# Two-layer decoder trunk: the end of the plain FFN columns as background streams, and the token sums in lanes of their own

## The chip, the cores and the metric

The kernel runs on one core of one Trainium2 chip. The metric is the time of one execution in microseconds (us), the median of three runs. All arithmetic is in 32-bit floats; the matmuls read them in a reduced fp32 form (fp32r), so every factor is split into a high and a low part and a product takes three passes.

## The reference

A trunk of two layers (l = 0, 1) works on 512 tokens of width 1024. In each layer stand an FFN half step (f = 0), a mixer, and another FFN half step (f = 1). The change touches the FFNs alone, and of these the part up to the first few of their 22 columns:

```
mod = c_act @ ada_w[l] + ada_b[l]          # nine vectors: shift, scale, gate
u = modulate(rmsnorm(h, ln_ffn), sh, sc)   # 512 x 1024
f = (silu(u @ w_gate) * (u @ w_up)) @ w_down     # 1024 -> 2816 -> 1024
h = h + 0.5 * gt * f
```

## The kernel before

**Tiling.** Activations stand transposed: 8 tiles of 128 features x 512 tokens. D_FF = 2816 is 22 columns of 128. Of the first columns of an FFN each is two plain products (`dense`: gate and up, 24 matmuls of 128x512 each, into one PSUM bank each, `mm`); the columns after them go in pairs by a scheme of seven products in place of eight (`dense_pair`), whose tokens stand in two halves of 256. A plain column ends in tanh on ACT (tile `t`), two VectorE instructions (`g` = (t+1)*gate, `ay` = g*up), and the split of `ay` into `ah` (a copy on ACT) and `al` (a subtraction on VectorE), which only the down product reads, behind the pairs.

**The pair.** Each of the seven jobs of `dense_pair` is 12 matmuls of 128x256: four k with the high parts, four with the low weight (`wl`), four with the low token part. The jobs use three banks X, Z and Y in the order X, Z, X, Y, X, Z, X. Jobs 1, 4 and 6 read `us` (the normalised tokens), jobs 2, 3, 5 and 7 read token sums `ts` (`th` high, `tl` low). After the first job ACT copies X into `c1` (in the trace `c<-mX`), and the third job, which overwrites X, waits for this copy.

**The token sums.** `halves_sums` makes them for k = 0 to 3: `make(0)` those of k = 0 and 2 on POOL, `make(1)` those of k = 1 and 3 on VectorE; per k four subtractions or additions and one sign change (`ta`, `tb`, 128x256), two copies on ACT (`th`, 128x512) and two subtractions on VectorE whatever the k (`tl`, 128x512). It is called at the end of `start()` (the first FFN; it also leaves the eight `mm` banks of four plain columns, `pss`) and of `tail()` (the others; two columns). The eight PSUM banks are all in use there, so the next `dense` needs a bank that one of these columns gives back: the first two banks are free when VectorE has done the column's two instructions.

**What sets the order.** The order on each engine is that in which the program text issues. After every third matmul (sixth in a pair) `tick()` makes one round through `lanes`, lists of generators, and steps those that a model clock calls due; in "post" it steps every due generator of the list, in the other lanes only the first due one. The lanes are gone through in the order in which the dictionary has them. `drain(names)` steps all lanes until the named ones are empty. The token sums stand in "post". `ffn()` begins with the four (or two) ready columns: all tanhs, all VectorE pairs, all splits. Then its loop goes through `seq`: for a "gu" column it makes the two `dense` and issues the column's end at once, in line; at the first "pair" it drains "post" and so the sums. In FFN (0,0) two plain columns (4 and 5) run in this loop, in the other three also two (2 and 3).

**Beside this** each weight tile is made into `wh` (copy on ACT) and `wl` (subtraction on VectorE) ahead of its use; POOL adds up weights of the pairs (`ws`); `ad`, `ca` and `ct` are the adaLN vectors, in work beside the FFNs.

Of the kernel before, what the change touches and what calls it, by code (L numbers as in the profile page):

```python
# [11 lines left out]
AF = mybir.ActivationFunctionType  # L12
OP = mybir.AluOpType
# [27 lines left out]
def ffn_order(first):  # L41


    seq = [("gu", i) for i in range(first)]
    nxt = first
    for ci, (lo, hi) in enumerate(CHUNKS):
        while nxt < min(hi + 1, FF):
            seq.append(("pair", nxt))
            nxt += 2
        seq.append(("down", ci))  # L50
    return seq


def first_gu(l, f):
    return 6 if (l, f) == (0, 0) else 4
# [3 lines left out]
def trunk(ctx: ExitStack, tc: tile.TileContext, x, c, ada_w, ada_b, ln, w_gu, w_dn, w_in, w_ba, conv_w,  # L59
# [17 lines left out]
    def big(s, shape=(128, 512), dt=F32):  # L77
        return bigp.tile(list(shape), dt, name=nm(s), tag="big")
# [46 lines left out]
    V, A, P, T = (Engine(k_, e_) for k_, e_ in zip("VAPT", (nc.vector, nc.scalar, nc.gpsimd, nc.tensor)))  # L125
# [43 lines left out]
    c_load()  # L169


    lanes = {"post": [], "dn0": [], "dn1": [], "at": []}

    def step(lane):

# [21 lines left out]
    def run(lane, gen):  # L197
        lanes[lane].append([gen, 0.0])
# [6 lines left out]
    def drain(*names):  # L205
        while any(lanes[n] for n in names):
            t = clock["T"]
            for n in lanes:
                step(n)
            if clock["T"] == t:  # L210
                clock["T"] += 100
# [380 lines left out]
            V.tensor_tensor(out=u[1][:, sl], in0=y, in1=u[0][:, sl].bitcast(F32), op=OP.subtract)  # L592
        return y, low

    def halves_sums(ys):

        lo, hi = HALF
        h12 = dnp.tile([128, 4, 2, 256], F32R, name=nm("th"), tag="MT")
        l12 = dnp.tile([128, 4, 2, 256], F32R, name=nm("tl"), tag="W")
        h34 = [dnp.tile([128, 2, 2, 256], F32R, name=nm("th"), tag=t_) for t_ in ("bt", "R")]  # L600
        ts = [[None] * 4 for _ in range(4)]

        l34 = [None] * 4

        def make(k0):
            for k in range(k0, 4, 2):
                l34[k] = big("tl", (128, 2, 256), F32R)
                for q, (th, tl) in enumerate(((h12[:, k], l12[:, k]), (h34[k // 2][:, k % 2], l34[k]))):
                    for i in range(2):
                        ts[2 * q + i][k] = (th[:, i, :], tl[:, i, :])  # L610
                E = (P, V)[k0]
                a, b = big("ta", (128, 2, 256)), big("tb", (128, 2, 256))
                y0, y1 = ys[k], ys[k + 4]
                E.tensor_tensor(out=a[:, 0, :], in0=y0[:, lo], in1=y0[:, hi], op=OP.subtract)
                E.tensor_tensor(out=a[:, 1, :], in0=y1[:, hi], in1=a[:, 0, :], op=OP.add)
                E.tensor_tensor(out=b[:, 1, :], in0=a[:, 1, :], in1=y1[:, lo], op=OP.subtract)
                yield
                E.tensor_scalar(out=a[:, 1, :], in0=a[:, 1, :], scalar1=-1.0, scalar2=None, op0=OP.mult)
                E.tensor_tensor(out=b[:, 0, :], in0=y1[:, hi], in1=y0[:, hi], op=OP.subtract)
                yield  # L620
                for t, th, tl in ((a, h12[:, k], l12[:, k]), (b, h34[k // 2][:, k % 2], l34[k])):
                    A.activation(out=th, in_=t, func=AF.Copy)
                    V.tensor_tensor(out=tl, in0=t, in1=th.bitcast(F32), op=OP.subtract)
                    yield

        for k0 in range(2):
            run("post", make(k0))
        return ts

    def pull(gen, n=1):  # L630
# [156 lines left out]
    def start(l, keys):  # L787
# [32 lines left out]
        y1s, us, ws, pss, ys = [], [], [], [], []  # L820
# [67 lines left out]
            V.tensor_tensor(out=sel, in0=sel, in1=ident[:, g:g + 16], op=OP.add)  # L888
        w_fill()
        w_ahead(12)  # L890
        return us, pss, halves_sums(ys)

    def split(y, s):
        hi, lo = big(s + "h", dt=F32R), big(s + "l", dt=F32R)
        A.activation(out=hi, in_=y, func=AF.Copy)
        V.tensor_tensor(out=lo, in0=y, in1=hi.bitcast(F32), op=OP.subtract)
        return hi, lo


    def ffn(l, f, us, pss, ts, nxt):  # L900
        act = {}
        st.update(ahead=AHEAD, raw=4)
        ada.update(rate=0.13, stop=min(len(ada_seq), 144 * l + 96 * f + 80))
        if (l, f) != (0, 0):
            ada["rate"] = 0.0
            c_load()

            def late():
                for _ in range(24):
                    yield False  # L910
                c_silu()
                ada["rate"] = 0.13

            run("post", late())
        seq = ffn_order(first_gu(l, f))

        def gate(cs, done):

            for c_, sign in zip(cs, (0.5, -0.5)):
                t = big("t")  # L920
                A.activation(out=t, in_=c_, func=AF.Tanh, scale=sign)
                yield
                V.scalar_tensor_tensor(out=c_, in0=t, scalar=1.0, in1=c_, op0=OP.add, op1=OP.mult)
                done.append(c_)
                yield

        def product(i, gs, done, ups):
            for j, (c_, y) in enumerate(zip(gs, ups)):
                while len(done) <= j:
                    yield False  # L930
                V.tensor_tensor(out=y, in0=c_, in1=y, op=OP.mult)
                yield
                act[i + j] = split(y, "a")
                yield
        gt = None
        there = [(pss[2 * i], pss[2 * i + 1]) for i in range(len(pss) // 2)]
        tanhs, ys = [big("t") for _ in there], [big("ay") for _ in there]
        for (pg, _), t in zip(there, tanhs):
            A.activation(out=t, in_=pg, func=AF.Tanh, scale=0.5)
        for (pg, pu), t, y in zip(there, tanhs, ys):  # L940
            V.scalar_tensor_tensor(out=t, in0=t, scalar=1.0, in1=pg, op0=OP.add, op1=OP.mult)
            V.tensor_tensor(out=y, in0=t, in1=pu, op=OP.mult)
        for i, y in enumerate(ys):
            act[i] = split(y, "a")
        for kind, i in seq[len(there):]:
            if kind == "gu":
                pg, pu = (dense(("gu", l, f, i, q), us) for q in range(2))
                t = big("t")
                A.activation(out=t, in_=pg, func=AF.Tanh, scale=0.5)
                g2 = big("g2")  # L950
                V.scalar_tensor_tensor(out=g2, in0=t, scalar=1.0, in1=pg, op0=OP.add, op1=OP.mult)
                y = big("ay")
                V.tensor_tensor(out=y, in0=g2, in1=pu, op=OP.mult)
                act[i] = split(y, "a")
            elif kind == "pair":
                if i == first_gu(l, f):
                    drain("post")
                g2s = dense_pair([("pair", l, f, j, 0) for j in (i, i + 1)], us, ts)
                done = []
                run("post", gate(g2s, done))  # L960
                ups = dense_pair([("pair", l, f, j, 1) for j in (i, i + 1)], us, ts)
                run("post", product(i, g2s, done, ups))
            else:
                if gt is None:
                    g_ = ada_need(l, 6 * f + 2)
                    gt = small("gt", [128, NF])
                    V.tensor_scalar(out=gt, in0=g_, scalar1=0.25, scalar2=None, op0=OP.mult)
                drain("post")
                lo, hi = CHUNKS[i]
                xs = [act.pop(j) for j in range(lo, hi)]  # L970
                last = i == len(CHUNKS) - 1
                st["ahead"] = 4 if last else AHEAD
                if last:
                    ada["rate"] = 0.0
                    Gs = gains(*nxt[:2]) if nxt else (None, None)
                    adds = []
                o = 0
                while o < (NF - TAIL if last else NF):
                    if last and o:
                        st["ahead"] = 3 + o  # L980
                    if last and o == 0:
                        pd = dense_late([("dn", l, f, i, q) for q in range(3)], xs)
                    else:
                        pd = [dense(("dn", l, f, i, o), xs)]
                    for p in pd:
                        V.scalar_tensor_tensor(out=h[o], in0=p, scalar=gt[:, o:o + 1], in1=h[o],
                                               op0=OP.mult, op1=OP.add)
                        if last:
                            norm_acc(o, adds)
                        o += 1  # L990
        return tail([("dn", l, f, i, q) for q in range(NF - TAIL, NF)], xs, gt, nxt, Gs, adds)
# [634 lines left out]
```

## Time and profile before

| what | value |
| --- | --- |
| time, median of three runs | 2740.14 us (2739.82, 2740.14, 2744.19) |
| profiled execution | 2742.23 us, its span 2740.4 us |
| mean granted TensorE clock | 0.993 |
| PE (matmul) | 2677.2 us busy, 98% |
| VectorE (DVE) | 2005.9 us, 73% |
| ScalarE (ACT) | 1286.4 us, 47% |
| GpSimd (POOL) | 867.1 us, 32% |

The table's busy times are from the page of the profiled execution. PE is the engine whose time is the span; what counts is where it stands idle, and what the clock does after that. The timeline's rows have a start in us from the span's start, a length, the engine, the line, the operation, its tiles with their shapes, how many instructions the row gathers (x4), and in brackets the idle time ahead of it with what ended it. All instructions that pass through the helper which keeps the model clock have line 122, so tiles tell them apart: `mX`, `mY`, `mZ` are the banks of a pair, `mm` that of a plain product.

### The profile page before, as it was taken

How to read it: one execution, taken by the hardware profiler on the slowest of the kernel's cores; microseconds unless marked ns; L12 is line 12 of the kernel's file. 1: busy time of each engine (PE TensorE's matmuls, PEld its weight loads, DVE VectorE, ACT ScalarE, POOL GpSimd, SP SyncE). 2: the span in 40 equal slices, each digit the busy share in tenths (PEclk: the TensorE clock that was granted, in tenths of full speed). 3: DMA queues.
4: the chain of work that ended last, by engine and by line, in shares of the span. 5: the costliest groups of instructions: out<-in, count | busy, mean ns of one | idle time of the engine just before them, and what ended most of it. 6: DMA issues, size and time to landing. Idle time of an engine off the chain costs nothing.

```text
span 2740.4 us, 48441 instructions
## 1 busy us (share of the span) xinstructions
PE 2677.2 (98%) x17332; PEld 2369.2 (86%) x17332; DVE 2005.9 (73%) x3889; ACT 1286.4 (47%) x2664; POOL 867.1 (32%) x1285
## 2 busy tenths in 40 slices
PE   6999999999999999999999999999999999999998
PEld 4899998878878888999989999888788888989997
DVE  8787878666655678888788877777665566787676
ACT  4454445555533335455544545445554333454453
POOL 4242314453450005223142232254345200234221
PEclk9999999999999999999999999999999999999999
DMA  8576632342344545777546766324323546266552
GB/s 285 155 217 193 165 110 94 105 130 76 103 136 158 170 141 148 222 200 194 145 110 199 217 198 166 108 68 122 97 69 106 156 160 216 93 179 175 149 144 66
DMA packets 254531, 407.13 MB, mean 149 GB/s; under 512 B 52817, under 2 KB 69969, under 8 KB 254289
## 3 DMA queue, kind: packets, MB, share of 16 engines
q1 hardware_dynamic: 231568, 358.93, 41.1%
q0 software_dynamic: 22720, 45.10, 9.2%
q8 instruction: 136, 2.23, 0.3%
q14 instruction: 107, 0.87, 0.1%
HBM read 382.95 MB, written 11.53 MB: 144 GB/s over the span
## 4 chain that ended last, share of the span: by engine, by line
PE 90%; DVE 4%; DMA 2%; ACT 2%; issue 1%; SPq 0%; POOL 0%; DVEq 0%; ACTq 0%
PE mm L122 53%; PE mX L122 13%; PE mZ L122 6%; PE tl L122 4%; PE mY L122 4%; PE as L122 1%; PE ob L122 1%; DVE ad L122 1%; PE pw L122 1%; PE pq L122 1%; PE aT L122 1%; PE po L122 1%; DVE wl L122 1%; DMA wr<-in_w_gu_dram 1%; ACT wh L122 1%
## 5 line engine op out<-in xcount | busy, mean ns | idle before, releaser
L122 DVE TENSOR_TENSOR wl<-wr,wh 128x512 fp32r<-128x512 f32 (+1 forms) x936 | 666.9, 747 | 157.3 <-ACT wh L122 154.9
L122 ACT ACTIVATE wh<-wr 128x512 fp32r<-128x512 f32 (+1 forms) x936 | 516.4, 595 | 139.0 <-PE mm L122 94.2
L122 PE MATMUL mm<-uh,wh 128*128 128x512 f32 (+1 forms) x1488 | 404.7, 379 | 11.8 <-ACT uh L122 11.8
L122 PE MATMUL mm<-uh,wl 128*128 128x512 f32 (+1 forms) x1488 | 404.4, 376 | 0.0
L122 PE MATMUL mm<-ul,wh 128*128 128x512 f32 (+1 forms) x1488 | 356.8, 374 | 1.6 <-DVE ul L122 1.6
L122 PEld LDWEIGHTS mm<-uh,wh 128*128 128x128 f32 x1488 | 272.8, 190 | 60.0 <-ACT uh L122 16.7
L122 PEld LDWEIGHTS mm<-uh,wl 128*128 128x128 f32 x1488 | 276.9, 190 | 43.4 <-issue 0.7
L122 PEld LDWEIGHTS mm<-ul,wh 128*128 128x128 f32 x1488 | 256.3, 189 | 44.0 <-DVE ul L122 2.3
L122 ACT ACTIVATE c<-mX 128x256 f32<-128x256 f32 x280 | 107.2, 383 | 320.6 <-PE mX L122 319.0
L293 POOL DMA_DIRECT2D wr<-in_w_gu_dram x70 | 61.7, 881 | 479.1 <-DVE wl L122 122.0
L122 DVE SCALAR_TENSOR_TENSOR ad<-ad,ca 128x512 f32<-128x512 f32 x272 | 191.5, 720 | 1.0 <-DMA ad<-in_ada_w_dram 0.8
L122 POOL TENSOR_SCALAR y<-y,G,mod 128x256 f32<-128x256 f32 (+1 forms) x88 | 65.0, 740 | 349.6 <-DVE y L122 322.5
L122 POOL TENSOR_TENSOR ws<-wr,wr 128x512 f32<-128x512 f32 x70 | 98.6, 1409 | 234.5 <-PE mm L122 68.4
L122 DVE TENSOR_TENSOR wl<-ws,wh 128x512 fp32r<-128x512 f32 x210 | 157.0, 754 | 9.9 <-ACT wh L122 6.2
L122 PE MATMUL mm<-ah,wh 128*128 128x512 f32 x608 | 160.0, 391 | 1.8 <-ACT wh L122 1.6
L122 PE MATMUL mm<-ah,wl 128*128 128x512 f32 x608 | 158.1, 389 | 0.0
L122 PE MATMUL mm<-al,wh 128*128 128x512 f32 x608 | 157.9, 389 | 0.0
L122 PE MATMUL mX<-th,wh 128*128 128x256 f32 x840 | 137.9, 287 | 14.1 <-ACT c L122 14.0
L122 DVE SCALAR_TENSOR_TENSOR h<-mm,gt,h 128x512 f32<-128x512 f32 x120 | 88.8, 747 | 75.1 <-PE mm L122 75.1
L122 PE MATMUL mX<-tl,wh 128*128 128x256 f32 x840 | 136.7, 286 | 0.0
L122 PE MATMUL mX<-th,wl 128*128 128x256 f32 x840 | 136.6, 285 | 0.0
L122 PEld LDWEIGHTS mm<-ah,wh 128*128 128x128 f32 x608 | 112.8, 188 | 27.6 <-ACT wh L122 3.3
(319 smaller groups left out, 5415.0 us busy)
## 6 DMA issues: line engine op xcount, KB each, us to landing
wr<-in_w_gu_dram SPq DMA_DIRECT2D x352, 256.0 KB, 4.5
ad<-in_ada_w_dram SPq DMA_DIRECT2D x288, 256.0 KB, 4.4
wr<-in_w_in_dram SPq DMA_DIRECT2D x264, 256.0 KB, 3.2
wr<-in_w_dn_dram SPq DMA_DIRECT2D x128, 256.0 KB, 3.0
ws<-in_w_gu_dram SPq DMA_DIRECT2D x70, 256.0 KB, 4.5
wr<-in_w_gu_dram POOLq DMA_DIRECT2D x70, 256.0 KB, 4.5
ws<-in_w_gu_dram POOLq DMA_DIRECT2D x70, 256.0 KB, 6.8
wr<-in_w_dn_dram SPq DMA_DIRECT2D x96, 128.0 KB, 3.2
```

The lines of the kernel that those rows point to most:

```text
L122: return fn(*args, **kw)
L293: nc.gpsimd.dma_start(out=out, in_=src, accum_op=OP.add)
```

## The change

Three things are changed, and no instruction is added or taken out on any engine. (1) The token sums get two lanes, "sum0" (POOL's k) and "sum1" (VectorE's k), ahead of "post"; at the first pair only these two are drained, no longer "post". (2) In `start()` VectorE's sums (`make(1)`) are issued at once, to their end, ahead of `ffn()`. (3) In the loop of `ffn()` the end of a plain column becomes a generator, `column`, in "post": one step issues the tanh, one the two VectorE instructions, one the split.

```
-    lanes = {"post": [], "dn0": [], "dn1": [], "at": []}
+    lanes = {"sum0": [], "sum1": [], "post": [], "dn0": [], "dn1": [], "at": []}
...
-    def halves_sums(ys):
+    def halves_sums(ys, now=False):
...
-        for k0 in range(2):
-            run("post", make(k0))
+        run("sum0", make(0))
+        run("sum1", make(1))
+        if now:
+            while lanes["sum1"]:
+                lanes["sum1"][0][1] = 0.0
+                step("sum1")
         return ts
...
-        return us, pss, halves_sums(ys)
+        return us, pss, halves_sums(ys, True)
...
+        def column(i, pg, pu):
+            t = big("t")
+            A.activation(out=t, in_=pg, func=AF.Tanh, scale=0.5)
+            yield
+            V.scalar_tensor_tensor(out=t, in0=t, scalar=1.0, in1=pg, op0=OP.add, op1=OP.mult)
+            y = big("ay")
+            V.tensor_tensor(out=y, in0=t, in1=pu, op=OP.mult)
+            yield
+            act[i] = split(y, "a")
...
             if kind == "gu":
                 pg, pu = (dense(("gu", l, f, i, q), us) for q in range(2))
-                t = big("t")
-                A.activation(out=t, in_=pg, func=AF.Tanh, scale=0.5)
-                g2 = big("g2")
-                V.scalar_tensor_tensor(out=g2, in0=t, scalar=1.0, in1=pg, op0=OP.add, op1=OP.mult)
-                y = big("ay")
-                V.tensor_tensor(out=y, in0=g2, in1=pu, op=OP.mult)
-                act[i] = split(y, "a")
+                run("post", column(i, pg, pu))
             elif kind == "pair":
                 if i == first_gu(l, f):
-                    drain("post")
+                    drain("sum0", "sum1")
```

The orders of PE, POOL and SP stay as they are; those of VectorE and ACT change at the start of the four FFNs. (In the rows below the numbers behind a tile's name count tiles and differ between the two kernels.)

VectorE at the start of FFN (0,0), before: the `wl` of the weights ahead, and then at once the two instructions of each ready column.

```order
L122 TENSOR_TENSOR wl_733<-wr_692,wh_732 128x512
L122 TENSOR_TENSOR wl_737<-wr_694,wh_736 128x512
L122 SCALAR_TENSOR_TENSOR t_750<-t_750,mm_258 128x512
L122 TENSOR_TENSOR ay_754<-t_750,mm_261 128x512
L122 SCALAR_TENSOR_TENSOR t_751<-t_751,mm_308 128x512
L122 TENSOR_TENSOR ay_755<-t_751,mm_361 128x512
```

The same place after: behind `wl_737` stand seven rows for k = 1 (the last of them is the first row here), the seven for k = 3, and then the columns.

```order
L122 TENSOR_TENSOR tl_750<-tb_752,th_748 128x512
L122 TENSOR_TENSOR ta_763<-y_382 128x256
L122 TENSOR_TENSOR ta_763<-y_652,ta_763 128x256
L122 TENSOR_TENSOR tb_764<-ta_763,y_652 128x256
L122 TENSOR_SCALAR ta_763<-ta_763 128x256
L122 TENSOR_TENSOR tb_764<-y_652,y_382 128x256
L122 TENSOR_TENSOR tl_747<-ta_763,th_746 128x512
L122 TENSOR_TENSOR tl_762<-tb_764,th_749 128x512
L122 SCALAR_TENSOR_TENSOR t_774<-t_774,mm_258 128x512
L122 TENSOR_TENSOR ay_778<-t_774,mm_261 128x512
```

The fourteen VectorE rows of `make(1)`, which stood among the rows up to the first pair, are now ahead of the instruction that frees the first bank (`t_774`).

ACT ahead of the first pair of FFN (0,0), before: the last plain column's tanh and copy, and behind them the copies of the sums, of k = 1 (`ta_797`), 0, 2 (`ta_1001`) and 3 (`ta_1015`).

```order
L122 ACTIVATE t_986<-mm_894 128x512
L122 ACTIVATE ah_992<-ay_990 128x512
L122 ACTIVATE th_748<-tb_792 128x512
L122 ACTIVATE th_746<-ta_797 128x512
L122 ACTIVATE th_746<-ta_1001 128x512
L122 ACTIVATE th_748<-tb_798 128x512
L122 ACTIVATE th_749<-tb_1002 128x512
L122 ACTIVATE th_746<-ta_1015 128x512
L122 ACTIVATE th_749<-tb_1016 128x512
```

After:

```order
L122 ACTIVATE t_997<-mm_902 128x512
L122 ACTIVATE th_748<-tb_816 128x512
L122 ACTIVATE ah_1004<-ay_980 128x512
L122 ACTIVATE ah_1008<-ay_1000 128x512
L122 ACTIVATE th_746<-ta_1013 128x512
L122 ACTIVATE th_749<-tb_1014 128x512
```

Only k = 2's copies are still behind the last column's `ah`; those of k = 1 and 3 stand some 20 rows further up, ahead of the ready columns' tanhs.

ACT around the first pair of FFN (0,1), before: `ah_12330` of the last plain column stands ahead of the copy of X.

```order
L122 ACTIVATE ct_12288<-ca_12095 128x512
L122 ACTIVATE ct_12291<-ca_12097 128x512
L122 ACTIVATE t_12324<-mm_12227 128x512
L122 ACTIVATE ah_12330<-ay_12328 128x512
L122 ACTIVATE wh_12340<-wr_12156 128x512
L122 ACTIVATE c_2890_12337<-mX_12334 128x256
```

After: the copy of X has no `ah` of the last column ahead of it, but that of the column before (`ah_12230`), which stands behind three `wh` now.

```order
L122 ACTIVATE wh_12203<-wr_11925 128x512
L122 ACTIVATE wh_12207<-wr_11931 128x512
L122 ACTIVATE wh_12211<-ws_2795_11937 128x512
L122 ACTIVATE t_12219<-mm_12115 128x512
L122 ACTIVATE ah_12230<-ay_12225 128x512
L122 ACTIVATE wh_12255<-wr_11926 128x512
L122 ACTIVATE wh_12259<-ws_2792_11929 128x512
L122 ACTIVATE wh_12263<-ws_2796_11938 128x512
L122 ACTIVATE wh_12267<-wr_11932 128x512
L122 ACTIVATE ct_12285<-ca_12093 128x512
L122 ACTIVATE ct_12288<-ca_12095 128x512
L122 ACTIVATE wh_12327<-wr_12154 128x512
```

Behind these come the last column's tanh and the copy of X; its `ah` comes six rows behind that copy. FFNs (1,0) and (1,1) are changed in the same way. VectorE there: three `wl` that stood behind the first plain column's `g`, `ay`, `al` now stand ahead of its `t`, `ay`.

## Rows read from the trace of the kernel before

**Rows 1.** The page, part 4: shares of the span in the chain that ended last, by engine.

```profile
PE 90%; DVE 4%; DMA 2%; ACT 2%; issue 1%; SPq 0%; POOL 0%; DVEq 0%; ACTq 0%
```

**Rows 2.** What PE waited for, over the whole span (waiting tile and line, what released it, its line: us in total, times, longest).

```profile
PE mX L122 <- ACT c L122: 14.0, 5, 5.2
PE mZ L122 <- ACT th L122: 5.5, 2, 4.6
```

**Rows 3.** Timeline of PE where it stands idle at the first pair of each FFN: (0,0), in the second job; then (0,1), (1,0) and (1,1), at the start of the third job.

```profile
104.49 0.90 PE L122 MATMUL mZ<-th,wh 128*128 128x256 f32 x2 [0.93 <-ACT th L122]
...
109.96 0.58 PE L122 MATMUL mZ<-th,wh 128*128 128x256 f32 x1 [4.57 <-ACT th L122]
...
1080.23 1.22 PE L122 MATMUL mX<-th,wh 128*128 128x256 f32 x4 [5.16 <-ACT c L122]
...
1436.70 1.22 PE L122 MATMUL mX<-th,wh 128*128 128x256 f32 x4 [3.81 <-ACT c L122]
...
2424.18 1.23 PE L122 MATMUL mX<-th,wh 128*128 128x256 f32 x4 [3.88 <-ACT c L122]
```

**Rows 4.** Busy time by stretch (from:to and length, busy us and instructions of PE, PEld, DVE, ACT, POOL, then the granted clock PEclk, the DMA share and GB/s): the stretches at and behind the four stalls, in their order, a stretch early in the program, and one in FFN (0,0).

```profile
108.10:114.60 6.50, 4.64 (x21) 4.64 (x22) 4.62 (x9) 3.36 (x7) 0.00 (x0) 0.50 0.26 81
1077.50:1084.30 6.80, 4.07 (x19) 4.07 (x20) 4.59 (x9) 3.83 (x9) 2.16 (x2) 0.50 0.41 134
1435.90:1442.70 6.80, 6.00 (x28) 6.00 (x29) 4.86 (x9) 3.48 (x8) 0.73 (x1) 0.50 0.61 196
2422.30:2429.20 6.90, 5.02 (x23) 5.02 (x24) 5.71 (x8) 4.15 (x9) 2.87 (x2) 0.51 0.48 133
36.40:39.80 3.40, 3.28 (x8) 2.63 (x9) 3.23 (x2) 2.17 (x6) 3.02 (x3) 0.50 1.05 386
138.00:142.00 4.00, 3.17 (x15) 2.29 (x14) 3.24 (x7) 3.45 (x8) 0.00 (x0) 1.00 0.93 342
```

**Rows 5.** Timeline of PE in the last two of these stretches: the shorter waits that stand there.

```profile
36.52 0.80 PE L122 MATMUL mm<-uh,wh 128*128 128x512 f32 x1 [2.15 <-ACT uh L122]
...
139.76 1.43 PE L122 MATMUL mm<-ah,wh 128*128 128x512 f32 x5 [0.83 <-ACT wh L122]
```

**Rows 6.** Timeline of ACT ahead of the third job in FFN (0,1).

```profile
1075.12 0.57 ACT L122 ACTIVATE t<-mm 128x512 f32<-128x512 f32 x1
1078.76 0.63 ACT L122 ACTIVATE ah<-ay 128x512 fp32r<-128x512 f32 x1 [3.07 <-DVE ay L122]
...
1079.82 0.36 ACT L122 ACTIVATE c<-mX 128x256 f32<-128x256 f32 x1
```

**Rows 7.** Timeline of VectorE in the same place: the end of the token sums, two of the weights' low parts, the last plain column's first instruction.

```profile
1067.79 0.68 DVE L122 TENSOR_TENSOR tl<-tb,th 128x512 fp32r<-128x512 f32 x1
...
1071.17 1.29 DVE L122 TENSOR_TENSOR wl<-wr,wh 128x512 fp32r<-128x512 f32 x2
...
1077.19 0.68 DVE L122 SCALAR_TENSOR_TENSOR g<-t,mm 128x512 f32<-128x512 f32 x1
```

**Rows 8.** FFN (1,0): the first plain column's first instruction and two of the weights' low parts on VectorE, two weight sums on POOL, the last column's copy on ACT.

```profile
1423.81 0.68 DVE L122 SCALAR_TENSOR_TENSOR g<-t,mm 128x512 f32<-128x512 f32 x1
...
1426.58 2.39 DVE L122 TENSOR_TENSOR wl<-wr,wh 128x512 fp32r<-128x512 f32 x2
...
1424.69 1.29 POOL L122 TENSOR_TENSOR ws<-wr,wr 128x512 f32<-128x512 f32 x1 [3.82 <-PE mm L122]
1426.06 1.76 POOL L122 TENSOR_TENSOR ws<-wr,ws 128x512 f32<-128x512 f32 x1
...
1435.22 0.63 ACT L122 ACTIVATE ah<-ay 128x512 fp32r<-128x512 f32 x1 [4.11 <-DVE ay L122]
```

**Rows 9.** FFN (0,0): VectorE's last weights, its first ready column, and the first and the last row of the sums of k = 3; ACT's copies at the stall; POOL's last weight sum and first token sum; PE's first plain product of the loop.

```profile
69.92 3.69 DVE L122 TENSOR_TENSOR wl<-wr,wh 128x512 fp32r<-128x512 f32 x6
79.22 0.69 DVE L122 SCALAR_TENSOR_TENSOR t<-t,mm 128x512 f32<-128x512 f32 x1 [5.60 <-ACT t L122]
...
107.59 0.41 DVE L122 TENSOR_TENSOR ta<-y 128x256 f32<-128x256 f32 x1
...
110.55 0.68 DVE L122 TENSOR_TENSOR tl<-tb,th 128x512 fp32r<-128x512 f32 x1
...
102.77 0.63 ACT L122 ACTIVATE ah<-ay 128x512 fp32r<-128x512 f32 x1 [5.11 <-DVE ay L122]
...
109.28 0.63 ACT L122 ACTIVATE th<-ta 128x512 fp32r<-128x512 f32 x1 [3.28 <-DVE ta L122]
...
74.84 1.29 POOL L122 TENSOR_TENSOR ws<-wr,ws 128x512 f32<-128x512 f32 x1
79.54 0.74 POOL L122 TENSOR_TENSOR ta<-y 128x256 f32<-128x256 f32 x1 [3.41 <-PE mm L122]
...
79.97 2.09 PE L122 MATMUL mm<-uh,wh 128*128 128x512 f32 x8
```

**Rows 10.** The sums of FFN (0,1), in which VectorE and POOL work at the same time: the first and the third instruction of VectorE's k = 1 and the first of its k = 3; POOL's weight sum ahead of its token sums.

```profile
1046.99 0.42 DVE L122 TENSOR_TENSOR ta<-y 128x256 f32<-128x256 f32 x1
...
1047.90 1.40 DVE L122 TENSOR_TENSOR tb<-ta,y 128x256 f32<-128x256 f32 x1
...
1053.70 0.61 DVE L122 TENSOR_TENSOR ta<-y 128x256 f32<-128x256 f32 x1
...
1047.56 1.45 POOL L122 TENSOR_TENSOR ws<-wr,wr 128x512 f32<-128x512 f32 x1 [2.77 <-PE mm L122]
```

## The prediction

> **What bounds the kernel now.** I read the chain of waits on the page first: PE holds 90% of it [rows 1], and with 2677.2 us busy of a span of 2740.4 only some 63 us are left in which PE stands. So the change can be worth only what lies in such gaps, and in the slow matmuls behind them. PE's waits by releaser name the gaps that are in its reach: five waits of a pair's third job for ACT's copy of X, 14.0 us, and two of the second job for a token sum, 5.5 us [rows 2]. The timeline puts them at the first pair of each FFN: 0.93 + 4.57 = 5.5 us at (0,0), call it place A; 5.16 at (0,1), B; 3.81 at (1,0), C; 3.88 at (1,1), D [rows 3]. The table by stretches shows the second price: behind each stall the granted clock is 0.50, that is 1.2 instead of 2.4 GHz, while PE is busy for 4.64, 4.07, 6.00 and 5.02 us [rows 4]; half of that is lost. So A costs 5.5 + 2.3 = 7.8 us, B 5.2 + 2.0 = 7.2, C 3.8 + 3.0 = 6.8, D 3.9 + 2.5 = 6.4: 28.2 us, 1% of the time. Shorter waits went either way: behind one of 0.83 us the clock stayed at 1.00, behind one of 2.15 it was 0.50 with PE busy for 3.28 us, 1.6 us lost [rows 4, 5].
>
> **Why B to D stall.** ACT's timeline shows it at B. The copy of X starts at 1079.82, and PE goes on 0.41 us later. Ahead of it stands the last plain column's `ah`, which started at 1078.76 after 3.07 us of idle [rows 6], because it needs `ay`, and VectorE came to that column's `g` only at 1077.19, behind the weights' low parts [rows 7]. At C ACT was idle for 4.11 us in the same place [rows 8], and D's stall has the same releaser [rows 3]. Nobody reads `ah` for many microseconds; the copy behind it holds PE.
>
> **The change at B, C and D.** The last column's `ah` now stands behind the copy of X, so this hold is gone. What is late next is the `ah` of the column before it, since three `wl` are put ahead of that column's `t` and `ay` on VectorE. At B: the last `tl` starts at 1067.79 and gives VectorE free at 1068.4; three `wl` at 0.60 (two take 1.29, rows 7) end at 1070.2; from `g` to the start of `ah` it took 1077.19 to 1078.76, 1.57 us [rows 6, 7], so `ah` starts at 1071.8. Between it and the copy of X ACT has nine starts (itself, five `wh`, two `ct`, the tanh), at (1079.82 - 1078.76) / 2 = 0.53 each: 4.8 us. The copy starts at 1076.6, PE at 1077.0. PE would be ready at 1080.23 - 5.16 = 1075.07, so a wait of 1.9 us is left. Does it take the clock down? It lies between 0.83 and 2.15 and is nearest to the latter, so I put 1.6 us on it, with 0 and 2.0 as ends. B is then 3.5 instead of 7.2: a gain of 3.7 (3.3 to 5.3).
>
> At C VectorE is free for the first `wl` at 1423.81, where the first column's `g` stood [rows 8]. Three `wl` and 1.57 us put `ah` at 1427.2. But POOL adds weights from 1424.69, and beside its next such sum (1.76 us) two `wl` took 2.39 instead of 1.29 [rows 7, 8]; I add 1.1, `ah` 1428.3, copy 1433.1, PE 1433.5. PE would be ready at 1436.70 - 3.81 = 1432.89: 0.6 us of wait, none without the collision. 0.6 is on the side of the 0.83 that left the clock alone. C gains 6.8 - 0.6 = 6.2. D has the same rows in the same order, and I carry the 0.6 over: 6.4 - 0.6 = 5.8. The streams' other instructions (the second column's `t`, `ay`, `ah`, `al`) come a few rows later on VectorE and ACT, which are busy for 73% and 47% of the span; their cover is the long way to the down product, so they cost nothing, and POOL's and SP's orders do not move.
>
> **The change at A.** Here the stall came from VectorE's sums of k = 3, made at 107.59 to 111.16 [rows 9], in the drain, with ACT's `th` at 109.28 behind them. They move up to 73.61, where VectorE was idle for 5.60 us. But PE's first plain product of the loop needs the bank that the first ready column's `t` gives back: `t` at 79.22, PE at 79.97, 0.75 us apart and with no idle on PE [rows 9]. All fourteen instructions now stand ahead of that `t`. Their price is the disputed number. Alone, one k takes 3.57 us [rows 9], two 7.2: VectorE is free at 80.8, PE starts at 81.5, 1.6 us late. Beside POOL one k took 1053.70 - 1046.99 = 6.7 us, with a 128x256 subtraction at 1.40 instead of 0.42 beside a weight sum of POOL [rows 10]. POOL is at work here too: its weight sum runs from 74.84 to 76.13, and its first token sums, which waited for PE until 79.54, no longer do, since the slots of their tiles now come from VectorE's early weights; five instructions at some 0.8 us reach about 80.2. So I take the first k beside POOL and the second alone: 73.6 + 6.7 + 3.6 = 83.9, PE at 84.7, a new wait of 4.7 us; the ends are 1.6 and, with both k beside POOL, 7.8. A wait of 4.7 is in the company of the four stalls: half clock, 2.3 us. At the old stall only POOL's k = 2 is left behind the last column's `ah` at 102.77: its copy starts 0.54 later and is done at 103.94, where PE wanted it at 104.49 - 0.93 = 103.56; with the next copy 0.5 us. A after: 4.7 + 2.3 + 0.5 = 7.5 instead of 7.8, a gain of 0.3 (from 5.7 at the lower end to -2.8). The stall is moved, not removed. VectorE's later start is made good by 7.2 us less to do on the way to the pair.
>
> **A rule against it.** The row of 1.40 us began at 1047.90 and ended just behind POOL's sum of 1047.56 + 1.45 = 1049.01 [rows 10]. This looks like standing still, not like sharing. The Trainium skill, SBUF — State Buffer, Who interferes with whom, says that VectorE and GpSimd share a port pair as an exclusive lock, and that a VectorE instruction with two SBUF inputs contends with a GpSimd instruction that reads SBUF; this row agrees.
>
> **The sum.** 0.3 + 3.7 + 6.2 + 5.8 = 16.0 us off the profiled execution of 2742.23 us: 2726.2. That execution is 2.1 us above the median of 2740.14, so 2724.1 for the median: 2724, 0.6% less.
>
> **Rivals.**
> (1) No collision at A. For it: POOL's sums might start later than I think. Against it: rows 10. A after 1.6 + 1.6 + 0.5 = 3.7, a gain of 4.1 instead of 0.3: 2720; if the short waits at A and B leave the clock up, 2717.
> (2) VectorE stands for everything that POOL does from 74.84 on, 1.29 + 5 x 0.8 = 5.3 us: sums to 80.8 + 5.3 = 86.1, PE 6.9 late, A after 9.7: 2726. The lock that the Trainium skill describes in the section named above, if it holds for every row here, gives this time.
> (3) The copy of X is still late: both of POOL's weight sums fall on the `wl` ahead of the first column, 2.2 us in place of what I took. B waits 4.1 and pays 2.0, C and D wait 1.7 and pay 1.6: gains 1.1, 3.5, 3.1, together with A 8.0: 2732.
> (4) Slower: VectorE runs late from A on. Sums at the slow rate throughout (7.8 late), half clock, and the delayed `ay` holds the last `ah` and so the old 5.5 + 2.3 at the second job: 17.9 instead of 7.8, +10.1. This makes the kernel slower only if B to D give less than 10.1 together; with nothing there it is 2750. Against it: VectorE has 7.2 us less to do before the pair, and A's wait does not reach B to D, which lie in other FFNs.
> That the change doesn't take place is no rival: the rows of the order show it at all four places.
>
> **How the numbers follow.** Forecast 0.45, rival (1) 0.20, (2) 0.12, (3) 0.15, (4) 0.03, and 0.05 that the freed time is taken by a later wait and nothing measurable is left. About 0.2%, 5.5 us, can be told from no change: under 2734.7 is faster. Faster is the first four, less a little of (3): 0.90; same 0.07; slower 0.03. The range reaches from rival (1) with the clock up, 2716, to a little over rival (3), 2733.
>
> **What will show it.** At A PE should stand before its first plain product of the loop, for about 4.7 us, released by VectorE's `t`, at half clock after that, and hardly any more at the second job; a POOL `ta` should start near 76 instead of 79.54. At B PE waits about 1.9 for ACT's copy, at C and D under 1, at a clock of 1.00 there. I am wrong if the wait at A is under 2 or over 7, if the copy of X still stalls PE for over 3 us at C or D, or if PE stands somewhere new in the rest of an FFN.

## The result, and the profile after

The changed kernel took 2724.76 us (median of 6 runs, 2722.66 to 2725.56), the kernel before beside it 2740.18 (2739.56 to 2744.47): ratio 0.9939, 95% interval 0.993 to 0.9949, 15.4 us less. 2724 was forecast. The profiled execution took 2723.15 us, its span is 2721.4, its mean granted clock 0.996. In the experiments below, one execution of the changed kernel (2920.19 us, at a clock of 0.85) and one of the kernel before (8187.23) stand far off all others, and the ratios leave them out.

What PE waited for in the changed kernel, as in [rows 2]:

```profile
PE mm L122 <- DVE t L122: 4.9, 1, 4.9
...
PE mX L122 <- ACT c L122: 2.7, 6, 0.5
```

The 14.0 us for the copy of X are down to 2.7, none over 0.5; the 5.5 us for `th` are 0.3 (the second row below); a wait of 4.9 us for VectorE's `t` is new. The timeline of PE shows it, with the rows that answer to [rows 3]: the first plain product of FFN (0,0), the second job of its first pair, then the third jobs of (0,1), (1,0) and (1,1):

```profile
84.39 3.78 PE L122 MATMUL mm<-uh,wh 128*128 128x512 f32 x8 [4.88 <-DVE t L122]
...
111.19 0.51 PE L122 MATMUL mZ<-th,wh 128*128 128x256 f32 x2 [0.29 <-ACT th L122]
...
1073.28 0.64 PE L122 MATMUL mZ<-tl,wh 128*128 128x256 f32 x4
1073.76 0.64 PE L122 MATMUL mX<-th,wh 128*128 128x256 f32 x4
...
1424.75 0.64 PE L122 MATMUL mX<-th,wh 128*128 128x256 f32 x4
...
2406.56 0.64 PE L122 MATMUL mX<-th,wh 128*128 128x256 f32 x4
```

PE stands for 4.88 us at 84.39, and at the three third jobs (`mX<-th,wh`) not at all: at (0,1) it starts 0.48 us behind the last group of the second job, which is the normal pace. The clock in these stretches (columns as in [rows 4]):

```profile
84.39:87.90 3.51, 3.51 (x8) 2.81 (x9) 3.25 (x6) 1.75 (x4) 1.48 (x2) 0.50 0.61 216
1071.00:1078.00 7.00, 7.00 (x61) 7.00 (x60) 6.89 (x11) 5.48 (x12) 3.47 (x3) 1.00 0.88 221
1422.00:1430.00 8.00, 8.00 (x69) 8.00 (x68) 7.90 (x13) 6.18 (x14) 4.17 (x4) 1.00 0.96 258
2404.00:2412.00 8.00, 8.00 (x69) 8.00 (x68) 7.89 (x12) 6.21 (x15) 4.27 (x4) 1.00 0.89 217
```

At 84.39 it is 0.50, at the other three 1.00. PE's 17,332 matmuls stand in the same order in both kernels, so the same matmul can be looked up in both timelines. Its start after less its start before, ahead of a place and behind it, and the difference of the two as the gain, in us:

| place | ahead of it | behind it | gain | forecast |
| --- | --- | --- | --- | --- |
| A, (0,0): from the first plain product of the loop to the pair's fourth job | -0.62 | -0.55 | -0.1 | 0.3 |
| B, (0,1): third job | -1.15 | -8.35 | 7.2 | 3.7 |
| C, (1,0): third job | -7.98 | -14.67 | 6.7 | 6.2 |
| D, (1,1): third job | -13.58 | -19.88 | 6.3 | 5.8 |
| last matmul | | -18.69 | | |

At A the wait came where it was expected. The slow matmuls behind it cost 2.8 us in this trace (12 of 128x512 at 0.43 us in place of 0.23). In two more traces of the same kernel (below) the wait is 4.9 us again, but only 5 and 6 matmuls are slow, 1.4 and 1.6 us, and A gains 1.4 and 1.1. Timeline of VectorE and POOL there: the first two instructions of k = 1, the first of k = 3, the first ready column; POOL's second weight sum and first token sum, which answer to [rows 9, 10]:

```profile
72.92 0.41 DVE L122 TENSOR_TENSOR ta<-y 128x256 f32<-128x256 f32 x1
73.36 1.40 DVE L122 TENSOR_TENSOR ta<-y,ta 128x256 f32<-128x256 f32 x1
...
79.49 0.61 DVE L122 TENSOR_TENSOR ta<-y 128x256 f32<-128x256 f32 x1
...
83.66 0.68 DVE L122 SCALAR_TENSOR_TENSOR t<-t,mm 128x512 f32<-128x512 f32 x1
...
74.56 1.35 POOL L122 TENSOR_TENSOR ws<-wr,ws 128x512 f32<-128x512 f32 x1
75.87 0.91 POOL L122 TENSOR_TENSOR ta<-y 128x256 f32<-128x256 f32 x1
```

VectorE's sums run from 72.92 to 83.66, 10.7 us against 7.2 alone, with the 128x256 addition at 1.40 beside POOL's weight sum, and the token sums of POOL start at 75.87, not at 79.54. At B it went otherwise than forecast. VectorE's last sum and first plain column, POOL's weight sum, ACT's first `ah` and the copy of X (before: [rows 6, 7]):

```profile
1064.12 0.68 DVE L122 TENSOR_TENSOR tl<-tb,th 128x512 fp32r<-128x512 f32 x1
...
1066.53 0.67 DVE L122 SCALAR_TENSOR_TENSOR t<-t,mm 128x512 f32<-128x512 f32 x1
...
1064.48 3.27 POOL L122 TENSOR_TENSOR ws<-wr,wr 128x512 f32<-128x512 f32 x1 [2.71 <-DVE tl L122]
...
1068.09 0.63 ACT L122 ACTIVATE ah<-ay 128x512 fp32r<-128x512 f32 x1 [2.90 <-DVE ay L122]
...
1072.75 0.37 ACT L122 ACTIVATE c<-mX 128x256 f32<-128x256 f32 x1
```

POOL's weight sum took 3.27 us, not 1.29, and VectorE's rows beside it kept 0.6 us each; `ah` started 4.66 us ahead of the copy of X, as worked out (4.8), and the copy was done in time.

### The profile page after: what moved, and what is told of

Its sections match the earlier page's. It is cut to its first block, busy times and chain, and to the rows that moved or that the text cites. A ratio compares the mean times of both kernels' runs of the same rounds, so it can differ in the third digit from the quotient of the medians.

```text
span 2721.4 us, 48452 instructions
## 1 busy us (share of the span) xinstructions
PE 2671.5 (98%) x17332; PEld 2362.5 (87%) x17332; DVE 2003.9 (74%) x3889; ACT 1285.0 (47%) x2664; POOL 872.9 (32%) x1285
## 4 chain that ended last, share of the span: by engine, by line
PE 92%; DVE 3%; issue 1%; ACT 1%; DMA 0%; SPq 0%; DVEq 0%; ACTq 0%
PE mm L122 54%; PE mX L122 14%; PE mZ L122 7%; PE tl L122 4%; PE mY L122 4%; PE as L122 1%; PE ob L122 1%; PE pw L122 1%; PE pq L122 1%; PE aT L122 1%; PE po L122 1%; DVE ad L122 1%; DVE c L122 1%; PE pm L122 1%; PE py L122 0%
## 5 line engine op out<-in xcount | busy, mean ns | idle before, releaser
L122 POOL TENSOR_TENSOR ws<-wr,wr 128x512 f32<-128x512 f32 x70 | 104.8, 1497 | 239.7 <-PE mm L122 53.3
```

The lines of the kernel that those rows point to most:

```text
L122: return fn(*args, **kw)
```

## The experiments

Each is a change to the changed kernel, with its diff against it. The first three undo one part each.

**The columns in line again.** The lanes and VectorE's sums at once are all that is left.

```
             if kind == "gu":
...
-                run("post", column(i, pg, pu))
+                t = big("t")
+                A.activation(out=t, in_=pg, func=AF.Tanh, scale=0.5)
+                g2 = big("g2")
+                V.scalar_tensor_tensor(out=g2, in0=t, scalar=1.0, in1=pg, op0=OP.add, op1=OP.mult)
+                y = big("ay")
+                V.tensor_tensor(out=y, in0=g2, in1=pu, op=OP.mult)
+                act[i] = split(y, "a")
```

> The changed kernel with the plain columns' ends issued in line again, so that only the lanes and VectorE's sums at once are left of the change. Theory (the gain is the three stalls at the third job of FFNs (0,1), (1,0) and (1,1), and the sums at once only move the stall of FFN (0,0)): those three stalls are back at 5.2, 3.8 and 3.9 us with the half clock behind them, PE waits some 4.9 us for VectorE's t in FFN (0,0), and the time is that of the kernel before, 2738 to 2742 us. Rival (the sums at once carry part of the gain): 2735 us or less.

2740.56 us (2737.46 to 2741.32) beside 2740.04: ratio 1.0 (0.9991 to 1.001). The waits for the copy of X are back, five with 14.0 us in all, and PE waits 4.9 us for VectorE's `t`:

```profile
PE mX L122 <- ACT c L122: 14.0, 5, 4.9
```

Over place A the same matmul's shift, taken as above, changes by 0.1 us. So the sums at once moved a stall and were worth nothing by themselves.

**The sums not at once.**

```
-        return us, pss, halves_sums(ys, True)
+        return us, pss, halves_sums(ys)
```

> The changed kernel without VectorE's sums at once: the sums stand in their lanes, the columns' ends are streams. Theory: B to D as in the changed kernel, no wait over 0.6 us there. In FFN (0,0) no wait for VectorE's t; the sums of k = 3 are made in the drain again, a few rows earlier than before, so a stall of 3 to 5 us at the second job with half clock behind it, 5 to 7.5 us in all against 7.5: 2722 to 2725 us, no more than 0.1% from the changed kernel. Rival (the sums at once were what the gain at (0,0) needed): the old 5.5 us wait with its slow clock and more behind it, 2728 us or over.

2725.83 us (2724.22 to 2729.67), ratio 0.9952 (0.994 to 0.9965). The median is 0.8 us over the band of the theory, with two sizes missed: the stall at A was not 3 to 5 us, and at B, where no wait over 0.6 us was expected, there was one of 1.74. The trace is that of the slowest of its five executions (2729.67). PE and VectorE at the second job:

```profile
111.34 0.58 PE L122 MATMUL mZ<-th,wh 128*128 128x256 f32 x1 [6.85 <-ACT th L122]
...
108.96 0.42 DVE L122 TENSOR_TENSOR ta<-y 128x256 f32<-128x256 f32 x1
```

PE stood 6.85 us (and 0.51 ahead of that), since VectorE came to the sums of k = 3 only at 108.96, and over place A 1.9 us were lost against the kernel before. So in the traces the sums at once are worth something beside the streams, where they keep A even; the times do not tell this kernel from the changed one (ratios 0.9952 and 0.9939, with intervals that overlap). At B the trace shows what had been forecast for the changed kernel. PE at the third job, the clock behind it (columns as in [rows 4]), VectorE, and POOL:

```profile
1079.22 0.74 PE L122 MATMUL mX<-th,wh 128*128 128x256 f32 x4 [1.74 <-ACT c L122]
...
1079.80:1083.20 3.40, 3.40 (x19) 3.40 (x18) 3.30 (x4) 1.90 (x5) 2.67 (x2) 0.50 0.07 23
...
1066.75 1.79 DVE L122 TENSOR_TENSOR tl<-tb,th 128x512 fp32r<-128x512 f32 x1
1068.47 1.78 DVE L122 TENSOR_TENSOR tl<-ta,th 128x512 fp32r<-128x512 f32 x1
...
1066.57 1.43 POOL L122 TENSOR_TENSOR ws<-wr,wr 128x512 f32<-128x512 f32 x1 [2.32 <-PE mm L122]
1068.08 1.62 POOL L122 TENSOR_TENSOR ws<-wr,ws 128x512 f32<-128x512 f32 x1
```

Two `tl` of VectorE took 1.79 and 1.78 us beside POOL's two weight sums at 1.43 and 1.62, PE waited 1.74 us for the copy of X, and behind the first four matmuls the granted clock was 0.50: a group of four took 0.85 us instead of 0.48. B gained 3.7 us, to the tenth what was worked out, with the order of instructions that the changed kernel has there.

**The old drain.** Streams and sums as in the changed kernel, but "post" is emptied at the first pair.

```
-                    drain("sum0", "sum1")
+                    drain("sum0", "sum1", "post")
```

> The changed kernel with the old drain at the first pair: the columns are streams and the sums are made at once, but post is emptied ahead of the first pair as well. VectorE's and ACT's rows ahead of the last plain column stay as in the changed kernel; the only thing that comes back is that column's ah ahead of the copy of X. Theory (what held PE at the third job of the last three FFNs is that ah): waits of 3.5 to 5.5 us with half clock behind them are back in all three, 18 to 21 us, so 2741 to 2746 us. Rival (the gain came from the streams' other moves, the three wl ahead of the first column and its ah behind them): at most 10 us come back, 2735 or less.

2738.11 us (2735.54 to 2740.92) beside 2739.84: ratio 0.9991 (0.9982 to 1.0). PE and ACT at B:

```profile
1079.79 1.18 PE L122 MATMUL mX<-th,wh 128*128 128x256 f32 x4 [3.12 <-ACT c L122]
...
1078.32 0.63 ACT L122 ACTIVATE ah<-ay 128x512 fp32r<-128x512 f32 x1 [3.00 <-DVE ay L122]
...
1079.38 0.37 ACT L122 ACTIVATE c<-mX 128x256 f32<-128x256 f32 x1
```

The last column's `ah` is ahead of the copy of X again, and PE waits 3.12 us, at C and D 3.18 and 3.09 (3.5 to 5.5 expected). The three places gain only 2.3, 0.6 and 0.3 us against the kernel before. Beside the changed kernel of the same chip (2722.93, below) 15.2 us come back, where 18 to 21 were expected, since the waits are shorter than before. Still, one line takes nearly all of the gain. That line is what made the streams pay: without it they are issued ahead of the pair anyway.

**POOL later.** POOL's first token sums are issued eight rounds later, so that their tiles lie in slots that VectorE's sums give back.

```
         def make(k0):
+            if now and k0 == 0:
+                for _ in range(8):
+                    yield False
             for k in range(k0, 4, 2):
```

> The changed kernel with POOL's first token sums in FFN (0,0) issued eight rounds later, so that their tiles' slots free only after VectorE's sums of k = 3: VectorE's fourteen instructions then meet POOL's weight sums alone. Theory (VectorE's sums were slowed by POOL's work beside them): the fourteen take 8.5 to 9.5 us instead of 10.7, PE waits 3 to 3.6 us instead of 4.9, half clock behind it as before: 1.5 to 2 us off, 2722.5 to 2723.5. Rival (their length is their own, from the copies on ACT that they wait for): 10.5 us or over, wait 4.9, time unchanged.

2720.86 us (2719.49 to 2721.79), ratio 0.9932 (0.992 to 0.9944). VectorE's first sum, the first of k = 3 and the first ready column, POOL's first token sum, PE:

```profile
73.48 0.42 DVE L122 TENSOR_TENSOR ta<-y 128x256 f32<-128x256 f32 x1
...
78.99 0.42 DVE L122 TENSOR_TENSOR ta<-y 128x256 f32<-128x256 f32 x1
...
82.64 0.68 DVE L122 SCALAR_TENSOR_TENSOR t<-t,mm 128x512 f32<-128x512 f32 x1
...
82.26 1.05 POOL L122 TENSOR_TENSOR ta<-y 128x256 f32<-128x256 f32 x1 [5.79 <-DVE tl L122]
...
83.37 3.61 PE L122 MATMUL mm<-uh,wh 128*128 128x512 f32 x8 [3.25 <-DVE t L122]
```

VectorE's fourteen took 9.2 us and PE waited 3.25, as expected; the time is 1.6 us under the band. k = 3, with no POOL beside it, took 3.65 us against 4.17 in the changed kernel, k = 1 5.5 against 6.6. So 1.6 us of A's 4.9 are the price of POOL's token sums. What still stands above the 1.6 us that the fourteen cost alone lies in k = 1, beside POOL's weight sums; that part is read from the rows and was not tried apart. Over place A this gains 2.8 us. That is more than the shorter wait, because the slow clock behind it was shorter too, 6 matmuls of 128x512 at the slow pace of 0.43 us against 12; but the changed kernel's two other traces have 5 and 6 behind the full wait, so this part is not the edit's.

**Only k = 1 at once.** The seven instructions that fit VectorE's idle time; k = 3 stays in its lane.

```
         if now:
-            while lanes["sum1"]:
+            for _ in range(4):
                 lanes["sum1"][0][1] = 0.0
                 step("sum1")
```

> The changed kernel with only the sums of k = 1 issued at once, those of k = 3 left to their lane. Theory (the new wait in FFN (0,0) is the fourteen instructions less the 5.6 us in which VectorE was idle): seven instructions take 3.6 to 6.6 us from 73 and fit into the idle time or miss it by under 1 us, so PE waits under 1 us for VectorE's t and the clock stays at 1.00; at the second job some 0.3 to 1 us. 6 to 7 us less than the changed kernel: 2717 to 2719.5 us. Rival (the wait is only put off to the second job, since k = 3 comes late again): a stall of 3 us or more there and half clock, 2722 to 2726.

2717.83 us (2716.36 to 2719.66), ratio 0.9921 (0.9907 to 0.9935). VectorE's first ready column, PE's first plain product, and PE's two waits at the second job, then the clock there:

```profile
79.53 0.69 DVE L122 SCALAR_TENSOR_TENSOR t<-t,mm 128x512 f32<-128x512 f32 x1 [0.25 <-ACT t L122]
...
80.28 2.10 PE L122 MATMUL mm<-uh,wh 128*128 128x512 f32 x8
...
104.76 0.50 PE L122 MATMUL mZ<-th,wh 128*128 128x256 f32 x2 [0.76 <-ACT th L122]
...
107.06 0.50 PE L122 MATMUL mZ<-tl,wh 128*128 128x256 f32 x2 [1.09 <-DVE tl L122]
```

```profile
103.00:110.00 7.00, 5.16 (x41) 4.75 (x40) 7.00 (x12) 5.37 (x12) 1.65 (x2) 1.00 0.15 44
```

No wait for `t`; 0.76 us for a `th` and 1.09 for a `tl` left the clock at 1.00. Place A gains 6.2 us.

**The rest of k = 3 at once too, behind the ready columns.** And, in a second kernel, all of VectorE's sums there. In both the forced steps stand between the columns' two instructions and their splits; the first has the diff above as well, the second calls `halves_sums(ys)`.

```
+        while (l, f) == (0, 0) and lanes["sum1"]:
+            lanes["sum1"][0][1] = 0.0
+            step("sum1")
         for i, y in enumerate(ys):
             act[i] = split(y, "a")
```

> The kernel with only k = 1's sums at once, and those of k = 3 issued at once too, but behind the two instructions of the four ready columns and ahead of their splits. Theory (what is left at (0,0) with k = 1 alone at once, 0.76 us for a th and 1.09 for a tl at the second job, is VectorE late on the way to the pair): no wait for VectorE's t, the tl wait goes, the th wait falls under 0.6 us; 1 to 1.5 us less than with k = 1 alone, 2716 to 2717.5. Rival (these waits come from POOL's k = 2, or VectorE is only later elsewhere): no gain, 2717.5 to 2720, or a new wait for a wl.

> The changed kernel with all of VectorE's sums in FFN (0,0) issued at once behind the two instructions of the four ready columns and ahead of their splits, so that VectorE's idle 5.6 us ahead of them stay unused. Theory (the sums must only be behind the instructions that give the banks back and ahead of the last plain column): no wait for VectorE's t, under 1 us at the second job at a clock of 1.00: 7 us less than the changed kernel, 2716 to 2719. Rival (the idle time is needed, VectorE gets late on the way to the pair): 2 us or more of wait for a wl or tl ahead of the pair or at its second job, 2720 to 2726.

2722.03 us (2721.13 to 2724.74), ratio 0.9931 (0.9919 to 0.9943), and 2726.17 (2723.96 to 2726.98), ratio 0.9942 (0.9929 to 0.9956). Both theories fell. The second kernel came out within 0.2 us of its rival (2720 to 2726), the first worse than its own (2717.5 to 2720). PE and VectorE of the second kernel:

```profile
110.45 0.79 PE L122 MATMUL mZ<-th,wh 128*128 128x256 f32 x2 [5.85 <-ACT th L122]
...
107.68 0.67 DVE L122 SCALAR_TENSOR_TENSOR t<-t,mm 128x512 f32<-128x512 f32 x1
```

VectorE came to the fifth column's `t` at 107.68, ACT's `ah` stood ahead of a `th`, and PE waited 5.85 us. In the first the two waits grew instead of falling. Its PE at the second job and the start of the third, and at D:

```profile
106.41 0.50 PE L122 MATMUL mZ<-th,wh 128*128 128x256 f32 x2 [1.49 <-ACT th L122]
...
108.98 0.51 PE L122 MATMUL mZ<-tl,wh 128*128 128x256 f32 x2 [1.35 <-DVE tl L122]
109.80 1.22 PE L122 MATMUL mX<-th,wh 128*128 128x256 f32 x4 [0.32 <-ACT c L122]
...
2408.45 0.74 PE L122 MATMUL mX<-th,wh 128*128 128x256 f32 x4 [1.46 <-ACT c L122]
```

VectorE's 5.6 idle us are needed: what is not done in them pushes the work behind, up to the pair. D had the slow form here that B has in the kernel with streams alone, with a `tl` and a `wl` at 1.77 us each beside POOL's sums.

**The sums' lanes stepped alone at the pair**, on top of k = 1 alone at once; and beside it that kernel and the changed one again, unchanged, on the same chip.

```
-                    drain("sum0", "sum1")
+                    while lanes["sum0"] or lanes["sum1"]:
+                        step("sum0")
+                        step("sum1")
+                        clock["T"] += 100
```

> The kernel with only k = 1's sums at once, and at the first pair the sums' two lanes stepped alone, so that the last plain column's stream is not stepped there and its ah no longer stands ahead of the copies of the last sums. Theory (what is left at (0,0) with k = 1 alone at once is the last column's work ahead of the sums): the waits of 0.76 us for th and 1.09 us for tl at the second job fall under 0.5 us each, FFNs (0,1) to (1,1) as with k = 1 alone at once: 1 to 2 us less than that kernel, 2715.5 to 2717. Rival (POOL's sums of k = 2 end late by themselves, and the column's ah now holds a later copy of the pair): no gain or up to 2 us more.

> The kernel with only k = 1's sums at once, again, on the same chip as the changed kernel beside it: 5 to 7 us less than that one, with no wait for VectorE's t in FFN (0,0). If the two are within 2 us of each other, what was seen between them came from the chips.

> The changed kernel beside the two above: 2722 to 2726 us, wait of 4.9 us for VectorE's t in FFN (0,0), no wait over 2 us at the third jobs.

2718.08 us (2717.12 to 2720.75; ratio 0.9922, 0.9908 to 0.9936), 2719.96 (2717.32 to 2723.53; 0.9926, 0.9913 to 0.9939) and 2724.4 (0.994, 0.9926 to 0.9954). The waits at the second job are gone in the first, but at the third and the fifth job PE waits for copies of X:

```profile
106.17 0.74 PE L122 MATMUL mX<-th,wh 128*128 128x256 f32 x4 [0.76 <-ACT c L122]
...
110.43 0.74 PE L122 MATMUL mX<-th,wh 128*128 128x256 f32 x4 [1.13 <-ACT c L122]
```

The rival held: the column's instructions now hold the pair's own copies, and the 1.9 us came back in another place. Between k = 1 alone and all at once the medians differ by 4.4 us on this chip, under the 5 to 7 expected, and the two intervals overlap; over place A the traces say 6.2 us of gain in both traces of the first against -0.1 to 1.4 in three of the second. In the medians (2717.83 and 2719.96 against 2722.93 to 2724.76) and in the traces k = 1 alone is the faster of the two; the intervals by themselves do not settle it.

**The changed kernel again**, without an edit, on the chip of the three kernels with the old drain and with k = 3 behind the columns.

> The changed kernel once more, beside the two above and for a second look at FFN (0,1), where the kernel with streams alone had a wait of 1.9 us and half clock at the third job, though its order there is the same, and the changed kernel had none. Theory (which of VectorE and POOL is held there depends on which starts first, and so on small shifts): both forms occur with this order; where POOL's first weight sum starts at least 10 us ahead of the third job, two tl of VectorE are slow and PE waits 1.5 to 2 us; where it starts later, POOL's sum takes 3 us or more and PE doesn't wait. Time 2722.5 to 2726.

2722.93 us (2722.31 to 2723.39), ratio 0.9932 (0.992 to 0.9945). POOL at B:

```profile
1064.55 4.38 POOL L122 TENSOR_TENSOR ws<-wr,wr 128x512 f32<-128x512 f32 x1 [2.21 <-DVE wl L122]
```

The rule that I gave fell: POOL's sum started 10.3 us ahead of the third job, and yet POOL was held, 4.38 us, and PE didn't wait. The slow form of B came in none of the changed kernel's three traces.

Which of the two came first does not tell the forms apart. At B, in both, POOL's sum came in the middle of a VectorE instruction, and VectorE's next one started 0.1 to 0.3 us behind it (kernel with streams alone: 1066.57, `tl` at 1066.75, slow; changed kernel: 1064.48, `wl` at 1064.72, at full pace). What differs in the rows is for how long VectorE's unbroken row of instructions with two SBUF inputs had run by then. At B to D of all thirteen traces POOL's first weight sum came thirty times into such a row with more of it to follow. Twice the row was 2.8 and 2.9 us old, and VectorE was slow (B before, and B with streams alone). In the other 28 it was 4.3 us old or more: in 27 POOL was held until VectorE's `t`, which reads PSUM (2.3 to 4.4 us for the sum), and once, at D with k = 3 at once too, VectorE was slow at 4.4. This is read from the traces; no experiment forced it, and why it is so stays open.

## Why the prediction was right, and where its terms were off

**What bounds, and where.** Right: the four places carry the gain, and the streams with the narrower drain are the mechanism at B to D. Streams alone keep the gain, columns in line lose it, the old drain loses it.

**A is even.** Right in its parts: wait 4.9 us (4.7 forecast), sums 10.7 us from 72.9 (10.3 from 73.6; k = 1 6.6 for 6.7, k = 3 4.2 for 3.6), slow clock behind it (2.8, 1.4 and 1.6 us in three traces for 2.3), 0.3 us left at the second job (0.5). The bounds were the two ends of one price, and the row with POOL beside it was the right one. The kernel with POOL later shows that 1.6 us of the wait are POOL's token sums, and the rows at 1.40 us reject rival (1). Rival (2), VectorE standing for all that POOL does, would have had PE 6.9 us late; with 4.9 it was too high, since POOL took its share of the delay: its five token sums took 0.88 to 1.16 us, not some 0.8.

**B was mis-sized**, 7.2 us for 3.7. The step that failed is "VectorE free at 1068.4": it carried over a trace in which two `tl` had been held by POOL's weight sums, from 1064.22 on:

```profile
1064.38 1.78 DVE L122 TENSOR_TENSOR tl<-tb,th 128x512 fp32r<-128x512 f32 x1
1066.09 1.77 DVE L122 TENSOR_TENSOR tl<-ta,th 128x512 fp32r<-128x512 f32 x1
```

In the changed kernel's three traces VectorE kept its pace there: twice POOL was held instead, once its sum came when VectorE was through. The kernel with streams alone had the forecast's form, and then the forecast's gain.

**C and D** gained 6.7 and 6.3 for 6.2 and 5.8. The 0.6 us put on a collision with POOL did not come, for the same reason: POOL was held, and no wait was left. Rival (3) would have needed VectorE to be held at both weight sums.

**"They cost nothing"** was wrong: in the next pair PE waits 0.3 to 0.6 us in seven of the nine places B to D of the three traces, which puts the same matmul back by 0.6 to 0.8 us each time. By the prediction's own sign (PE standing somewhere new in the rest of an FFN) this is a miss, though a small one. At C, PE's third job there, VectorE, ACT:

```profile
1435.40 0.74 PE L122 MATMUL mX<-th,wh 128*128 128x256 f32 x4 [0.41 <-ACT c L122]
...
1431.47 0.68 DVE L122 TENSOR_TENSOR al<-ay,ah 128x512 fp32r<-128x512 f32 x1
...
1434.45 0.63 ACT L122 ACTIVATE t<-c 128x512 f32<-128x512 f32 x1 [1.40 <-DVE c L122]
1434.98 0.36 ACT L122 ACTIVATE c<-mX 128x256 f32<-128x256 f32 x1
```

The last column's `al` is among what VectorE does ahead of the pair's `c`; so the next `t` on ACT waits for `c`, and the copy of X behind it is late by 0.41 us. This is read from the rows and was not tried apart; a `wl` and an `ad` ahead of that `al` took 1.78 us each from 1428.05 on, some 2.2 us more than at full pace, which would do it as well. One more wait, of 1.7 us for a copy of X, stands at 193 us in two of the changed kernel's three traces, 0.6 before; its cause is open.

**The sum** of 16.0 fits 15.4, 16.9 and 16.4 us in three comparisons of medians, but partly by luck, since errors offset each other: B to D gave 20.2 us in the trace where 15.7 was forecast, and the later waits and shifts in the mixers took 2 us of that back (-0.62 ahead of A less 20.1 at the four places is -20.7; the last matmul stands at -18.7). The two profiled executions lie 19.1 us apart, and not 16.0; that of before is 2.1 us above its median, that of after 1.6 below, which leaves the 15.4.

## What to carry to other kernels

An instruction whose result nobody needs soon, but which waits in an in-order queue ahead of one that somebody does, can cost its whole wait; make it a background stream, and look whether a drain ahead of the critical part issues it there anyway. Work moved into an engine's idle time pays up to the length of that idle time: seven of the fourteen instructions fitted, the other seven put the stall ahead of the next bank. And before a time of VectorE or POOL is carried over from a trace, look whether the other was at work beside it in that trace: the same rows in the same order came out both ways here.

## What the runs showed of the hardware

- VectorE and POOL hold each other up: two `tl` took 1.79 and 1.78 us for 0.68, or a weight sum of POOL 3.27 and 4.38 for 1.29. The Trainium skill, SBUF — State Buffer, Who interferes with whom, says that issue order decides who blocks. The traces agree where `tl` started 0.2 us behind POOL's sum and stood (kernel with streams alone). They do not agree where POOL was held: in the changed kernel three VectorE instructions that started behind POOL's sum ran ahead of it, and it waited through the whole row of instructions with two SBUF inputs, up to the next that reads PSUM.
- The clock after a wait of PE is not told by the wait's length alone in these rows: behind 1.74 us at B (streams alone) it was 0.50, behind 1.46 us at D (k = 3 at once too) 1.00, and in the same kernel behind 1.49, 1.35 and 0.32 us close together 0.50. A single wait of 1.67 us at 193 us, in the second trace of the changed kernel, left it at 1.00.
